# A unit's score products of both heads in one block, and a priority for the sum of its values, in the sparse attention of a decoder

## The chip, the cores and the metric

One Trainium2 chip, one core. The metric is the device time of one execution in microseconds (us), as the median of several runs. Engines are called as in the profile: PE is the matrix engine and PEld its weight loads, DVE the vector engine, ACT the scalar engine, POOL the GpSimd engine.

## The reference, cut to what matters

A decoder of two layers, 512 tokens of 1024 features, all in float32. Each layer has a half-step feed-forward block, a mixer and another half-step feed-forward block. The mixer of the first layer is a gated linear recurrence beside an mLSTM, that of the second is a sparse attention with three branches. Only the attention matters here:

```python
sc = jnp.einsum('bqgrd,bngd->bgrqn', qb, kc)              # compressed keys
p_cmp = masked_softmax(sc, cmp_end[None, :] <= t[:, None])
o_cmp = jnp.einsum('bgrqn,bngd->bqgrd', p_cmp.astype(vc.dtype), vc)
...
ss = jnp.einsum('bqgrd,bgqkd->bgrqk', qb, k_sel)          # selected keys
p_slc = masked_softmax(ss, sel_mask)
o_slc = jnp.einsum('bgrqk,bgqkd->bqgrd', p_slc.astype(v_sel.dtype), v_sel)
...
sw = jnp.einsum('bqgrd,bkgd->bgrqk', qb, k_win)           # a window of 256 keys
p_win = masked_softmax(sw, win_mask)
o_win = jnp.einsum('bgrqk,bkgd->bqgrd', p_win.astype(v_win.dtype), v_win)
out = gb[..., 0:1] * o_cmp + gb[..., 1:2] * o_slc + gb[..., 2:3] * o_win
```

There are 4 groups of 4 heads with 64 features each. With 512 tokens all 8 blocks of 64 keys are selected, so the selected branch is causal attention over all keys.

## The kernel before

Every product in float32 is made of three products of a shorter format: each operand is split into a high and a low half, and high x high, high x low and low x high are added in psum (`mm3`, L175 to L177). PE's order is the order in which the code issues its instructions (`tc.manual_schedule` for PE alone). ACT, DVE and POOL are ordered by a scheduler, by the priorities that follow from the order of the code; `tc.high_priority(offset=...)` puts what it holds that many steps ahead. Each engine then works through its own list in order.

The attention (`nsa`) goes through 32 units: 4 groups `g`, 4 blocks `qb` of 128 queries, and `par`, which picks two of the group's four heads, r = 0 and 1. The work of a unit has two parts.

`scores(u)` makes the scores of both heads. For one head (`both(r)`) these are four products. Two have 128 rows: the high half of the query stands on 64 of them and its low half on the other 64, so that one product against the high half of the keys covers two of the three terms (L942 for the selected keys in `p1`, L943 for the window and the compressed keys together in `p2`). Two have 64 rows: the query's high half against the keys' low half (L944, L945). A `psum()` tile has one of five banks. Then `soft` runs three times, for selected, window and compressed keys: a DVE operation adds the mask and finds the extreme (L932), and an ACT exponential follows (L934), which sums too. `last` also makes the factors `cf` (L952, L953) with which POOL scales the probabilities (L960, L961).

`outputs(u)` multiplies with the values. In a `turn` PE transposes up to four blocks of probabilities into a psum tile `px` (L984), ACT copies it as the high half `ph` (L988), and DVE subtracts for the low half `pl` (L989). In the `add` that belongs to it PE multiplies the values with both (L1000, L1001), with 32 rows for the compressed branch. The `add` comes one turn late. `px` and the accumulator `po` share a pool of three banks. After the last `add` of a unit ACT copies half of `po` to the other half of the partitions (`o`, L1011), DVE adds (L1012), and for every second unit DVE and POOL split the sum (L1016, L1017).

The loop goes over units n: it makes the `outputs` of unit n, and between their turns it hands out the scores of unit n+2 and the fillers, evenly mixed in one list `items`. A filler is three products 512 wide, one step of a projection that the attention needs later (queries and keys first, 69 steps, then 32 steps of the output projection of the first heads). A step of scores is one entry of the list that `scores` returns, so in the kernel before the two heads are two entries with fillers and turns between them:

```python
                    while sc or fl:
                        items += fl[:1] + sc[:1]
                        sc, fl = sc[1:], fl[1:]
```

Of the kernel before, what the change touches and what calls it, by code (L numbers as in the profile page):

```python
# [9 lines left out]
AF = mybir.ActivationFunctionType  # L10
OP = mybir.AluOpType

P = 128
# [41 lines left out]
def build(tc, a, out, stages=("f0a", "ab", "f0b", "f1a", "nsa", "f1b")):  # L55
    nc = tc.nc
    with ExitStack() as ctx:
# [16 lines left out]
        def blk(i, dt, name):  # L74
            return bp.tile([P, BW.get(i, 4 * T)], dt, name=name, tag=f"b{i}")

        def slots(blocks, dt, name):
            return [t[:, s * T:(s + 1) * T] for t in (blk(b, dt, f"{name}{b}") for b in blocks) for s in range(4)]
# [5 lines left out]
        def psum():  # L84
            return pp.tile([P, T], F32, name="ps", bufs=PSB)

        def psum2():
            return pp.tile([P, T], F32, name="pt", bufs=8 - PSB)
# [624 lines left out]
        def nsa(x, nxt):  # L713
# [3 lines left out]
            KH = slots((4,), F32R, "kh")  # L717
            b5, b6, b7 = (blk(b, F32R, f"k{b}") for b in (5, 6, 7))
            KL = [b5[:, m * T:(m + 1) * T] for m in range(2)]
            VC = b5[:, 2 * T:3 * T].rearrange("p (g e) -> p g e", g=NG)  # L720
            kw = [t[:, n * 576:(n + 1) * 576] for t in (b6, b7) for n in range(3)]
            KWH, KWL = kw[0:4], kw[4:6]
# [187 lines left out]
            def scores(u):  # L910
                g, qb, par = u
                qs = slice(qb * P, (qb + 1) * P)
                rr = half[g % 2]
                nk = (qb + 1) * P
                nw = min(3, qb + 1) * P
                w0, wwin, wcmp = (160, 0, 384) if qb == 3 else (0, 32, 0)
                n1, n2 = max(256, nk), max(256, nw + 32)
                mx = tp.tile([P, 2, 3], F32, name="mx", bufs=4)
                sm = tp.tile([P, 2, 3], F32, name="sm", bufs=4)
                cf = tp.tile([P, 2, 3], F32, name="cf", bufs=4)  # L920
                pc = PC[cnt[0] % len(PC)]
                cnt[0] += 1
                Pu = room(u, 2 * (nk + nw))
                pt = [(pc[:, r], Pu[:, r * (nk + nw):r * (nk + nw) + nk], Pu[:, r * (nk + nw) + nk:(r + 1) * (nk + nw)])
                      for r in range(2)]

                def soft(r, b, src, msk):
                    dst = pt[r][b]
                    put = dst
                    if len(msk.shape) == 3:  # L930
                        put, src = (v.rearrange("p (b n) -> p b n", n=P) for v in (dst, src))
                    nc.vector.tensor_tensor_reduce(out=put, in0=src, in1=msk, scale=1.0, scalar=3e38,  # L932
                                                   op0=OP.add, op1=OP.min, accum_out=mx[:, r, b:b + 1])
                    nc.scalar.activation(dst, dst, AF.Exp, scale=-1.0, bias=mx[:, r, b:b + 1],  # L934
                                         accum_out=sm[:, r, b:b + 1])

                def both(r):
                    q = QH[g][2 * r + par]  # L940
                    p1, p2 = psum(), psum()
                    nc.tensor.matmul(p1[:, :n1], q[:, qs], KH[g][:, :n1], start=True, stop=False)  # L942
                    nc.tensor.matmul(p2[:, :n2], q[:, qs], KWH[g][:, w0:w0 + n2], start=True, stop=False)  # L943
                    nc.tensor.matmul(p1[:, :n1], q[rr, qs], KL[g // 2][rr, :n1], start=False, stop=True)  # L944
                    nc.tensor.matmul(p2[:, :n2], q[rr, qs], KWL[g // 2][rr, w0:w0 + n2], start=False, stop=True)  # L945
                    soft(r, 1, p1[:, :nk], MS[:, T - nk:])
                    soft(r, 2, p2[:, wwin:wwin + nw], MS[:, T - nw:] if qb < 2 else MW)
                    soft(r, 0, p2[:, wcmp:wcmp + 32], MC[:, qb])

                def last():  # L950
                    both(1)
                    nc.vector.reciprocal(cf, sm)  # L952
                    nc.vector.tensor_mul(cf, cf, gate[:, qb, 12 * g:12 * g + 12]  # L953
                                         .rearrange("p (r s b) -> p r s b", s=2, b=3)[:, :, par])
                    if qb == 0:
                        nc.vector.tensor_mul(cf[:, :, 0], cf[:, :, 0], valid0)
                    for b in (1, 2):
                        for r in range(2):
                            w = pt[r][b].shape[1]
                            nc.gpsimd.tensor_mul(pt[r][b], pt[r][b], cf[:, r, b:b + 1].to_broadcast([P, w]))  # L960
                    nc.gpsimd.tensor_mul(pc, pc, cf[:, :, 0:1].to_broadcast([P, 2, 32]))  # L961

                probs[u] = pt
                return [lambda: both(0), last]


            def outputs(u):
                g, qb, par = u
                qs = slice(qb * P, (qb + 1) * P)
# [5 lines left out]
                parts, po = {}, []  # L975
# [18 lines left out]
                def add(n):  # L994
                    if n == 0:
                        po.append(psum2())
                    kk, ph, pl = parts.pop(n)
                    for m, (_, v, _) in enumerate(pairs[n]):
                        ms = slice(m * 2 * P, (m + 1) * 2 * P)
                        nc.tensor.matmul(po[0][:, :2 * P], v, ph[:kk, ms], start=n == 0 and m == 0, stop=False)  # L1000
                        nc.tensor.matmul(po[0][:, :2 * P], v, pl[:kk, ms], start=False,  # L1001
                                         stop=n == len(pairs) - 1 and m == len(pairs[n]) - 1)
                    if n < len(pairs) - 1:
                        return
                    if g not in OB:
                        OB[g] = blk((12, 13, 0, 1)[g], F32R, f"o{g}")[:, :4 * T].rearrange("p (k t) -> p k t", k=4)

                    if par == 0:
                        sums[0] = tp.tile([P, 2 * P], F32, name="o", bufs=1)
                    o, own, oth = sums[0], half[par], half[1 - par]  # L1010
                    nc.scalar.activation(o[own], po[0][oth, :2 * P], AF.Copy)  # L1011
                    nc.vector.tensor_add(o[own], po[0][own, :2 * P], o[own])  # L1012
                    if par == 1:
                        oh, ol = OB[g][:, 0:2, qs], OB[g][:, 2:4, qs]
                        o = o.rearrange("p (k t) -> p k t", k=2)
                        nc.vector.tensor_copy(oh, o)  # L1016
                        nc.gpsimd.tensor_sub(ol, o, oh.bitcast(F32))  # L1017
# [97 lines left out]
        last = []  # L1115
# [4 lines left out]
        with tc.manual_schedule(engines=PE_ONLY):  # L1120
            for _ in range(10):
                nc.tensor.matmul(ps[:, :P], ident, ident, start=True, stop=True)
        w0 = [tuple(wp.tile([P, CW], dt, name=nm, bufs=b) for nm, dt, b in
                    (("raw", F32, 2), ("whi", F32R, None), ("wlo", F32R, None))) for _ in range(2)]
# [21 lines left out]
        for n, st in enumerate(stages):  # L1146
# [17 lines left out]
            else:  # L1164
                f = {"f0a": 0, "f0b": 1, "f1a": 2, "f1b": 3}[st]
# [107 lines left out]
```

## Time and profile before

| | before |
| --- | --- |
| median of 3 runs | 2093.01 us |
| runs | 2088.83, 2093.01, 2098.58 us |
| profiled execution | 2106.2 us |
| its span in the trace | 2104.5 us |
| PE busy | 2014.4 us (96%) |
| DVE, ACT, POOL busy | 1383.4 us (66%), 1027.8 us (49%), 280.0 us (13%) |
| mean granted clock of PE | 0.976 |

The profiled execution is one more run, a little longer than those timed. The times in the rows are microseconds from its start. Its attention units run from about 1459 to 1705 us, some 245 us of the whole. Busy time of PE is modelled at the ends of products, so the distance from one start to the next says more than a product's own duration, and a busy PE may still be showing a weight load that isn't hidden.

### The profile page before, as it was taken

What the parts mean: (1) busy time and instruction counts of PE and PEld (TensorE: products, weight loads), DVE (VectorE), ACT (ScalarE), POOL (GpSimd) and SP (SyncE); (2) the same over time, 40 slices, a digit from 0 to 9 for tenths busy, and PEclk for the clock granted to TensorE, in tenths of its full rate; (3) what the DMA queues carried; (4) which work ended last, traced back from release to release, by engine and by line L of the source; (5) the groups of instructions that cost most, each with busy time, mean ns of one, the idle gap of its engine ahead of it and who ended that gap; (6) DMA issues with size and microseconds to landing.
All of it is one profiled execution on the core that took longest, in us unless ns stands there. A gap on an engine that the chain in (4) does not pass through costs nothing.

```text
span 2104.5 us, 30561 instructions
## 1 busy us (share of the span) xinstructions
PE 2014.4 (96%) x11896; PEld 1750.7 (83%) x11896; DVE 1383.4 (66%) x2189; ACT 1027.8 (49%) x1900; POOL 280.0 (13%) x290
## 2 busy tenths in 40 slices
PE   7999899989999999999999999999999999999997
PEld 5889898767888998897889989877777677999896
DVE  6847647488568657475865747433777788657474
ACT  4525436445445435254544525424877755435252
POOL 3000000243020000002000000201646440000002
PEclk9999999999899999999999999999999999999998
DMA  5232322222132323233232323321000032323212
GB/s 172 74 115 83 111 85 76 90 81 90 61 101 80 109 82 111 76 98 108 79 113 83 107 88 99 121 90 60 31 21 17 31 106 80 102 89 111 85 61 85
DMA packets 74737, 182.10 MB, mean 87 GB/s; under 512 B 8416, under 2 KB 9184, under 8 KB 74592
## 3 DMA queue, kind: packets, MB, share of 16 engines
q1 hardware_dynamic: 74448, 180.06, 27.6%
q8 instruction: 93, 1.52, 0.3%
q14 instruction: 52, 0.43, 0.1%
q10 hardware_dynamic: 144, 0.09, 0.0%
HBM read 178.02 MB, written 2.10 MB: 86 GB/s over the span
## 4 chain that ended last, share of the span: by engine, by line
PE 72%; DVE 12%; DMA 6%; issue 5%; ACT 3%; POOL 0%; SPq 0%; DVEq 0%; POOLq 0%; ACTq 0%
PE ps L175 17%; PE ps L176 17%; PE ps L177 17%; DMA r<-wgu 6%; PE pt L176 3%; PE pt L175 3%; PE pt L177 3%; PE px L984 2%; PE pt L779 2%; DVE wlo L319 1%; PE pt L1000 1%; DVE wx L319 1%; DVE r L309 1%; DVE r L310 1%; PE ps L944 1%
## 5 line engine op out<-in xcount | busy, mean ns | idle before, releaser
L169 ACT ACTIVATE whi<-raw 128x1024 fp32r<-128x1024 f32 (+2 forms) x196 | 193.3, 988 | 374.4 <-PE ps L176 254.5
L176 PE MATMUL ps<-h,whi 128*128 128x512 f32 x704 | 278.9, 396 | 0.7 <-DVE h L390 0.7
L175 PE MATMUL ps<-h,whi 128*128 128x512 f32 x704 | 277.8, 395 | 0.7 <-ACT h L389 0.7
L177 PE MATMUL ps<-h,wlo 128*128 128x512 f32 x704 | 277.2, 394 | 0.0
L318 ACT ACTIVATE whi<-r 128x1024 fp32r<-128x1024 f32 (+1 forms) x174 | 165.8, 953 | 211.2 <-PE ps L176 171.0
L170 DVE TENSOR_TENSOR wlo<-raw,whi 128x1024 fp32r<-128x1024 f32 (+2 forms) x166 | 192.5, 1162 | 78.7 <-ACT whi L169 73.8
L116 POOL TENSOR_TENSOR acc<-acc,t 128x512 f32<-128x512 f32 x48 | 76.9, 1603 | 1149.4 <-ACT t L114 1144.2
L457 DVE SCALAR_TENSOR_TENSOR X<-ps,X 128x512 f32<-128x512 f32 x96 | 66.4, 691 | 238.1 <-PE ps L177 238.1
L319 DVE TENSOR_TENSOR wlo<-r,whi 128x1024 fp32r<-128x1024 f32 (+1 forms) x174 | 189.1, 1088 | 28.1 <-ACT whi L318 27.8
L175 PE MATMUL ps<-x,whi 128*128 128x512 f32 x432 | 179.4, 415 | 6.0 <-ACT whi L1133 6.0
L176 PE MATMUL ps<-x,whi 128*128 128x512 f32 x432 | 171.0, 396 | 5.1 <-DVE x L105 4.9
L309 DVE TENSOR_TENSOR r<-r,r 128x1024 f32<-128x1024 f32 x72 | 89.4, 1242 | 130.5 <-DMA r<-wgu 130.4
L177 PE MATMUL ps<-x,wlo 128*128 128x512 f32 x432 | 171.3, 396 | 0.1
L175 PEld LDWEIGHTS ps<-h,whi 128*128 128x128 f32 x704 | 133.7, 190 | 30.8 <-ACT h L389 1.2
L176 PEld LDWEIGHTS ps<-h,whi 128*128 128x128 f32 x704 | 133.7, 190 | 30.7 <-DVE h L390 2.1
L177 PEld LDWEIGHTS ps<-h,wlo 128*128 128x128 f32 x704 | 133.7, 190 | 29.3
L175 PE MATMUL ps<-qB,whi 128*128 128x256 f32 x520 | 145.8, 280 | 2.8 <-ACT u L363 2.8
L177 PE MATMUL ps<-qB,wlo 128*128 128x256 f32 x520 | 145.2, 279 | 1.0 <-DVE wlo L319 1.0
L176 PE MATMUL ps<-qB,whi 128*128 128x256 f32 x520 | 145.3, 279 | 0.1
L319 DVE TENSOR_TENSOR wx<-r,wx 128x1024 fp32r<-128x1024 f32 (+1 forms) x114 | 125.1, 1098 | 23.6 <-ACT wx L318 21.1
L389 ACT ACTIVATE h<-t 128x512 fp32r<-128x512 f32 x88 | 55.4, 630 | 145.3 <-DVE t L371 143.1
L318 ACT ACTIVATE wx<-r 128x1024 fp32r<-128x1024 f32 (+1 forms) x114 | 107.5, 943 | 11.4 <-DVE r L309 9.1
(340 smaller groups left out, 5500.4 us busy)
## 6 DMA issues: line engine op xcount, KB each, us to landing
r<-wgu SPq DMA_DIRECT2D x288, 256.0 KB, 3.7
raw<-wd SPq DMA_DIRECT2D x64, 512.0 KB, 3.5
raw<-wgu SPq DMA_DIRECT2D x30, 512.0 KB, 3.6
raw<-wd SPq DMA_DIRECT2D x32, 384.0 KB, 3.1
raw<-ab_fm SPq DMA_DIRECT2D x21, 512.0 KB, 3.5
raw<-nsa_fm SPq DMA_DIRECT2D x17, 512.0 KB, 3.5
raw<-ab_out SPq DMA_DIRECT2D x8, 512.0 KB, 3.6
raw<-nsa_out SPq DMA_DIRECT2D x16, 256.0 KB, 2.7
```

The source lines that it names most:

```text
L116: nc.gpsimd.tensor_add(acc, acc, sq)
L169: nc.scalar.activation(hi[:, :n], raw[:, :n], AF.Copy)
L170: (eng or nc.vector).tensor_sub(lo[:, :n], raw[:, :n], hi[:, :n].bitcast(F32))
L175: nc.tensor.matmul(ps, wh, xh, start=start, stop=False, skip_group_check=on)
L176: nc.tensor.matmul(ps, wh, xl, start=False, stop=False, skip_group_check=on)
L177: nc.tensor.matmul(ps, wl, xh, start=False, stop=stop, skip_group_check=on)
L309: nc.vector.tensor_add(ra[:, 1:3], ra[:, 0:4:3], rc[:, 3:4].to_broadcast([P, 2, T]))
L318: nc.scalar.activation(hi[:, :m], src, AF.Copy)
L319: nc.vector.tensor_sub(lo[:, :m], src, hi[:, :m].bitcast(F32))
L389: nc.scalar.activation(hh, t2, AF.Copy)
L457: nc.vector.scalar_tensor_tensor(X[i], ps, 0.5, X[i], op0=OP.mult, op1=OP.add)
L779: nc.tensor.matmul(p2[m][:, :155].rearrange("p (g n) -> p g n", g=5), w[:, q * 256 + m * P:q * 256 + (m + 1) * P], tt[:, :, n:n + 8 * 30 + ...
```

## The change

Two edits, both in `nsa`. In `scores`, a unit's two heads are made in one step instead of two, and the products are ordered so that the four with 64 rows stand together: the first head has its 128-row products first, the second head its 64-row products. In `outputs`, the ACT copy and the DVE addition of the sum get a priority 60 steps ahead.

```diff
@@ -939,15 +939,20 @@
                 def both(r):
                     q = QH[g][2 * r + par]
                     p1, p2 = psum(), psum()
-                    nc.tensor.matmul(p1[:, :n1], q[:, qs], KH[g][:, :n1], start=True, stop=False)
-                    nc.tensor.matmul(p2[:, :n2], q[:, qs], KWH[g][:, w0:w0 + n2], start=True, stop=False)
-                    nc.tensor.matmul(p1[:, :n1], q[rr, qs], KL[g // 2][rr, :n1], start=False, stop=True)
-                    nc.tensor.matmul(p2[:, :n2], q[rr, qs], KWL[g // 2][rr, w0:w0 + n2], start=False, stop=True)
+                    for n, f in enumerate((0, 1) if r == 0 else (1, 0)):
+                        a, z = n == 0, n == 1
+                        if f == 0:
+                            nc.tensor.matmul(p1[:, :n1], q[:, qs], KH[g][:, :n1], start=a, stop=z)
+                            nc.tensor.matmul(p2[:, :n2], q[:, qs], KWH[g][:, w0:w0 + n2], start=a, stop=z)
+                        else:
+                            nc.tensor.matmul(p1[:, :n1], q[rr, qs], KL[g // 2][rr, :n1], start=a, stop=z)
+                            nc.tensor.matmul(p2[:, :n2], q[rr, qs], KWL[g // 2][rr, w0:w0 + n2], start=a, stop=z)
                     soft(r, 1, p1[:, :nk], MS[:, T - nk:])
                     soft(r, 2, p2[:, wwin:wwin + nw], MS[:, T - nw:] if qb < 2 else MW)
                     soft(r, 0, p2[:, wcmp:wcmp + 32], MC[:, qb])
 
                 def last():
+                    both(0)
                     both(1)
                     nc.vector.reciprocal(cf, sm)
                     nc.vector.tensor_mul(cf, cf, gate[:, qb, 12 * g:12 * g + 12]
@@ -961,7 +966,7 @@
                     nc.gpsimd.tensor_mul(pc, pc, cf[:, :, 0:1].to_broadcast([P, 2, 32]))
 
                 probs[u] = pt
-                return [lambda: both(0), last]
+                return [last]
 
 
             def outputs(u):
@@ -1008,8 +1013,9 @@
                     if par == 0:
                         sums[0] = tp.tile([P, 2 * P], F32, name="o", bufs=1)
                     o, own, oth = sums[0], half[par], half[1 - par]
-                    nc.scalar.activation(o[own], po[0][oth, :2 * P], AF.Copy)
-                    nc.vector.tensor_add(o[own], po[0][own, :2 * P], o[own])
+                    with tc.high_priority(offset=60):
+                        nc.scalar.activation(o[own], po[0][oth, :2 * P], AF.Copy)
+                        nc.vector.tensor_add(o[own], po[0][own, :2 * P], o[own])
                     if par == 1:
                         oh, ol = OB[g][:, 0:2, qs], OB[g][:, 2:4, qs]
                         o = o.rearrange("p (k t) -> p k t", k=2)
```

The lines move: L942 to L945 become L945, L946, L948 and L949; L984, L988 and L989 become L989, L993 and L994; L1000 and L1001 become L1005 and L1006; L1011 and L1012 become L1017 and L1018.

On PE, at the scores of the last unit of the second group (512 selected keys; `kh4`, `k6` are high halves of keys, `k5`, `k7` low halves, `t1` and `t2` high and low halves of transposed probabilities, `v8` and `v9` values), before:

```order
L942 MATMUL ps_13862<-kh4_11882,q11_12696 128x512
L943 MATMUL ps_13863<-k6_11884,q11_12696 128x416
L944 MATMUL ps_13862<-k5_11883,q11_12696 128x512
L945 MATMUL ps_13863<-k7_11885,q11_12696 128x416
L1000 MATMUL pt_13782<-t1_13825,k5_11883 128x256
L1001 MATMUL pt_13782<-t2_13826,k5_11883 128x256
L984 MATMUL px_13879<-ident_80,pb14_11888 128x128 x4
L175 MATMUL ps_13854<-x0_11658,whi_13850 128x512
L176 MATMUL ps_13854<-x2_11660,whi_13850 128x512
L177 MATMUL ps_13854<-x0_11658,wlo_13851 128x512
L1000 MATMUL pt_13893<-t1_13844,v8_11886 128x256
L1001 MATMUL pt_13893<-t2_13845,v8_11886 128x256
```

and after:

```order
L945 MATMUL ps_13845<-kh4_11882,q11_12740 128x512
L946 MATMUL ps_13846<-k6_11884,q11_12740 128x416
L948 MATMUL ps_13845<-k5_11883,q11_12740 128x512
L949 MATMUL ps_13846<-k7_11885,q11_12740 128x416
L948 MATMUL ps_13857<-k5_11883,q11_12740 128x512
L949 MATMUL ps_13858<-k7_11885,q11_12740 128x416
L945 MATMUL ps_13857<-kh4_11882,q11_12740 128x512
L946 MATMUL ps_13858<-k6_11884,q11_12740 128x416
L1005 MATMUL pt_13795<-t1_13819,k5_11883 128x256
L1006 MATMUL pt_13795<-t2_13820,k5_11883 128x256
L989 MATMUL px_13881<-ident_80,pb14_11888 128x128 x4
L175 MATMUL ps_13701<-x1_11659,whi_13697 128x512
```

The second head's four products, which came after another block of value products and transposes, now stand directly behind the first head's, with the four 64-row products in the middle; the 32-row value products and the transposes `px_13881` come after all eight.

On ACT, from the copy of `o` at the same place on (`pb14` to `pb16` hold probabilities), before:

```order
L1011 ACTIVATE o_13876<-pt_13782 64x256
L988 ACTIVATE t1_13884<-px_13879 128x512
L934 ACTIVATE pb15_11889,sm_13837<-pb15_11889,mx_13836 128x512
L934 ACTIVATE pb15_11889,sm_13837<-pb15_11889,mx_13836 128x384
L934 ACTIVATE pb16_11890,sm_13837<-pb16_11890,mx_13836 128x32
L988 ACTIVATE t1_13903<-px_13898 128x512
L882 ACTIVATE q11_13858<-t1_13859 64x512
L887 ACTIVATE q11_13858<-t1_13859 64x512
L882 ACTIVATE q11_13858<-t1_13859 64x512
L934 ACTIVATE pb15_11889,sm_13837<-pb15_11889,mx_13836 128x512
```

and after, from the copy of the transposes ahead of the scores on:

```order
L993 ACTIVATE t1_13838<-px_13833 128x512
L934 ACTIVATE pb15_11889,sm_13831<-pb15_11889,mx_13830 128x512
L1017 ACTIVATE o_13878<-pt_13795 64x256
L934 ACTIVATE pb15_11889,sm_13831<-pb15_11889,mx_13830 128x384
L934 ACTIVATE pb16_11890,sm_13831<-pb16_11890,mx_13830 128x32
L934 ACTIVATE pb15_11889,sm_13831<-pb15_11889,mx_13830 128x512
L934 ACTIVATE pb15_11889,sm_13831<-pb15_11889,mx_13830 128x384
L934 ACTIVATE pb16_11890,sm_13831<-pb16_11890,mx_13830 128x32
L993 ACTIVATE t1_13886<-px_13881 128x512
L993 ACTIVATE t1_13903<-px_13898 128x512
```

Before, the copies of the transposes `px_13879` and `px_13898` stand ahead of and between the exponentials of the two heads. After, the six exponentials of both heads stand in a row with only the copy of `o` among them, and the copies of `px_13881` and `px_13898` behind the last.

On DVE, at the same place (an L932 row without names reads the accumulator), before:

```order
L932 ISA pb15_11889,mx_13836<-ps_13862,masks_11891 128x512
L932 ISA mx_13836 128x1
L932 ISA pb15_11889,mx_13836<-ps_13863,masks_11891 128x384
L932 ISA mx_13836 128x1
L932 ISA pb16_11890,mx_13836<-ps_13863,pb15_11889 128x32
L932 ISA mx_13836 128x1
L1012 TENSOR_TENSOR o_13876<-pt_13782,o_13876 64x256
L989 TENSOR_TENSOR t2_13885<-px_13879,t1_13884 128x512
L989 TENSOR_TENSOR t2_13904<-px_13898,t1_13903 128x512
```

and after:

```order
L932 ISA pb15_11889,mx_13830<-ps_13845,masks_11891 128x512
L932 ISA mx_13830 128x1
L932 ISA pb15_11889,mx_13830<-ps_13846,masks_11891 128x384
L932 ISA mx_13830 128x1
L932 ISA pb16_11890,mx_13830<-ps_13846,pb15_11889 128x32
L932 ISA mx_13830 128x1
L932 ISA pb15_11889,mx_13830<-ps_13857,masks_11891 128x512
L932 ISA mx_13830 128x1
L1018 TENSOR_TENSOR o_13878<-pt_13795,o_13878 64x256
L932 ISA pb15_11889,mx_13830<-ps_13858,masks_11891 128x384
L932 ISA mx_13830 128x1
```

The addition of `o`, which stood behind the three steps of one head, now stands behind four of six steps and ahead of the last two, and the subtractions for the low halves of the following transposes have moved behind all of them.

## Rows read from the trace of the kernel before

**Rows 1.** Attention's stretch: us; busy PE, PEld, DVE, ACT, POOL (instructions); clock; DMA; GB/s

```profile
1455.00:1710.00 255.00, 244.93 (x1350) 186.16 (x1349) 191.84 (x663) 194.52 (x585) 134.81 (x190) 0.99 0.10 31
```

**Rows 2.** Sums of waits from 1455 to 1705: engine, who waits, releaser; us, times, longest

```profile
PE px L984 <- DVE o L1012: 5.8, 10, 1.1
...
PEld px L984 <- DVE o L1012: 4.9, 7, 1.1
...
PE pt L1000 <- DVE t L989: 1.9, 2, 1.7
```

**Rows 3.** Timeline of PE, scores between fillers: start, duration, line, operation, shapes [idle before]

```profile
1461.43 0.28 PE L942 MATMUL ps<-kh,q 128*128 128x256 f32 x1
1461.55 0.28 PE L943 MATMUL ps<-k,q 128*128 128x256 f32 x1
1461.76 0.38 PE L944 MATMUL ps<-k,q 64*128 64x256 f32 x1
1461.98 0.28 PE L945 MATMUL ps<-k,q 64*128 64x256 f32 x1
1462.19 0.50 PE L175 MATMUL ps<-x,whi 128*128 128x512 f32 x1
1462.53 0.39 PE L176 MATMUL ps<-x,whi 128*128 128x512 f32 x1
1462.76 0.40 PE L177 MATMUL ps<-x,wlo 128*128 128x512 f32 x1
```

**Rows 4.** Timeline of PE around the unit at 1568.87

```profile
1568.87 0.40 PE L942 MATMUL ps<-kh,q 128*128 128x512 f32 x1
...
1569.38 0.50 PE L944 MATMUL ps<-k,q 64*128 64x512 f32 x1
...
1570.22 0.27 PE L1001 MATMUL pt<-t,k 32*128 32x256 f32 x1
...
1572.78 0.66 PE L984 MATMUL px<-ident,pb 128*128 128x128 f32 x4 [0.54 <-DVE o L1012]
1573.19 0.48 PE L942 MATMUL ps<-kh,q 128*128 128x512 f32 x1
...
1574.41 0.50 PE L175 MATMUL ps<-x,whi 128*128 128x512 f32 x1
...
1575.20 0.28 PE L1000 MATMUL pt<-t,v 128*128 128x256 f32 x1
```

**Rows 5.** Timeline of ACT around the same unit

```profile
1570.59 0.38 ACT L1011 ACTIVATE o<-pt 64x256 f32<-64x256 f32 x1 [0.77 <-PE pt L1001]
...
1571.83 0.72 ACT L934 ACTIVATE pb<-pb,mx 128x512 f32<-128x512 f32 x1
...
1572.55 0.60 ACT L934 ACTIVATE pb<-pb,mx 128x384 f32<-128x384 f32 x1
...
1573.53 0.60 ACT L988 ACTIVATE t<-px 128x512 fp32r<-128x512 f32 x1
```

**Rows 6.** Groups by line and form, 1459 to 1705: busy us, mean ns, idle before

```profile
L984 PEld LDWEIGHTS px<-ident,pb 128*128 128x128 f32 x304 | 34.1, 141 | 11.6 <-DVE o L1012 3.8 <-POOL pb L960 2.4 <-POOL pb L961 1.3
```

**Rows 7.** Timeline of DVE around the same unit

```profile
1569.94 1.25 DVE L953 TENSOR_TENSOR cf<-cf,pb 128x6 f32<-128x6 f32 x1
1571.11 0.68 DVE L932 CUSTOM_DVE_ANT_0 pb<-ps,masks 128x512 f32<-128x512 f32 x1
...
1572.31 0.41 DVE L1012 TENSOR_TENSOR o<-pt,o 64x256 f32<-64x256 f32 x1
...
1574.16 0.69 DVE L989 TENSOR_TENSOR t<-px,t 128x512 fp32r<-128x512 f32 x1 [0.84 <-ACT t L988]
```

**Rows 8.** Timeline of PE, two waits for the low half of a transposed block

```profile
1594.74 0.38 PE L1000 MATMUL pt<-t,v 128*128 128x256 f32 x1 [0.19 <-DVE t L989]
...
1667.44 0.39 PE L1000 MATMUL pt<-t,v 128*128 128x256 f32 x1 [1.68 <-DVE t L989]
```

**Rows 9.** Busy time behind the second of them, columns as in rows 1

```profile
1669.60:1673.20 3.60, 3.60 (x13) 2.54 (x12) 2.91 (x9) 1.07 (x3) 1.24 (x2) 0.53 0.23 73
```

## The prediction

> **What bounds the kernel now.** The page's table of busy time comes first: PE is the one full engine. Only the sparse attention of the second layer is touched, so next comes the table of busy time for that stretch, 1455 to 1710 us: PE 244.93 of 255 us, ACT 194.52, DVE 191.84, the granted clock at 0.99 [rows 1]. PE bounds this stage too, but ACT and DVE are at about 76%, and each hands PE an operand several times per unit. So the time of the change is what it takes from or adds to PE's own work, and how often PE waits for ACT and DVE. The sums of waits give today's sizes: PE waits 5.8 us, in ten places, for the sum of a unit's values (`o`, L1012), its load engine another 4.9 us, and 1.9 us for the low half of a transposed block (`t`, L989) [rows 2]. The timeline of PE gives the price of the short products, and the timelines of three engines around one unit give the chain that the change rearranges; there the reader is to see who stands in front of whom.
>
> **The change part by part: the weight loads.** In the timeline of PE a 128-row product of 256 columns behind another starts 0.12 us after it (1461.43 to 1461.55) [rows 3]: its weight load is hidden. From there to the 64-row product it is 0.21 us, to the second 0.22, to the filler behind it 0.21, each 0.09 to 0.10 more; and the filler's first product is 0.34 us from its second (1462.19 to 1462.53), where the second is 0.23 from the third. So a run of two 64-row products shows four loads of about 0.10 us: before it, within it, after it, and one more. A run of four shows six. Two runs of two become one of four in each of 32 units: 8 loads become 6, that is 64 fewer. In 17 places of the order of before, a run stands directly ahead of the 32-row products of the compressed values, which shows the same cost, so the two shared it; in the order of after the 32-row products come behind 128-row ones and pay it alone, two loads each, 34 in all. 64 - 34 = 30 fewer, at 0.10 us: **-3.0 us**. The Trainium skill, page "TensorEngine Tiling (Array Packing)", section "Key Properties", says that a change of the tiling mode drains TensorE. By that rule alone only the changes would cost, 64 fewer of them less 17 that were shared, 47 at 0.10 us or -4.7 us, and the time about 2100, inside the range of the forecast. The row of the second 64-row product, 0.22 us without any change of rows, speaks against that rule being all of it.
>
> **The sum of values.** `o` takes an ACT copy and a DVE addition, and transposes behind it wait, because they take the psum bank that it frees. In the unit at 1568.87 the copy starts at 1570.59, the addition comes behind the softmax steps of the head just scored, at 1572.31, and PE sits idle 0.54 us until 1572.78 [rows 4, 5, 7]. These waits are 5.8 us in PE alone and 10.7 us with those of the load engine [rows 2]. I take a value near the lower end, since the loads mostly run beside PE and only one of 0.141 us [rows 6] stands exposed behind each of the ten: 5.8 + 10 x 0.14 = 7.2 us. With the new priority the addition stands ahead of the last softmax steps of 384 and 32 columns, and in nearly every unit of the new order PE has more work between the last value product and the waiting transposes than the copy and the addition need. I find only three places where it has less, for 0.4 us together: **-6.8 us**. The bounds are -10.7 (both engines' waits, all gone) and 0 (PE waits for the copy instead).
>
> **The copies of transposed blocks, the new cost.** Before, scores of one head were followed by other work, so that ACT had three exponentials, then copies of transposed blocks (L988), then three more. Now all six scores of a unit come at once, the scheduler puts all six exponentials in a row on ACT, and the copies of the transposes that PE issues right behind the scores stand behind them. ACT takes them in that order. I work it out for the unit at 1568.87 (the second order excerpt), in time from its first score product:
> - The 64-row product that ends the first softmax input starts at 0.51 and lasts 0.50, so the softmax step can start at 1.0; in before it started at 2.2 (1571.11), behind an operation of 1.25 us on DVE [rows 4, 7]. The exponential follows 0.72 later (1571.83): at 1.7 to 3.0.
> - Four products and the two 32-row ones reach 1.35 (1568.87 to 1570.22); the other four add about 1.2 (1573.19 to 1574.41) less a load, so the second 32-row product starts at 2.5 and ACT's copy of `o` 0.37 behind it (1570.22 to 1570.59), at 2.9 [rows 4, 5].
> - From one exponential to the next it is 0.72 us behind the one of 512 keys, and 0.98 for those of 384 and 32 together (1571.83, 1572.55, 1573.53) [rows 5]. In the early case the copy of `o` (about 0.4) falls behind the first exponential, and five more follow it (0.98 + 0.72 + 0.98 = 2.7): the copy of the transposed block starts at 6.0. In the late case all six stand there, to 6.6.
> - The low half starts 0.63 later (1573.53 to 1574.16) and takes 0.69 [rows 5, 7]: PE has its operand at 7.3 to 7.9.
> - PE gets there, without waits, in the time between the same two products of before (1570.22 to 1575.20), less the second run of scores (1.2) and the idle 0.54: 3.2 us behind 2.5, and the first product that takes the low half is one product on, at 5.8 [rows 4].
> So PE waits some 1.5 to 2.1 us, where it waited for nothing in before; I take 1.6, since the operation of 1.25 us isn't there in every unit. The same working at each of the 32 units, with exponentials of their widths, gives a wait at 14: seven of the eight units with 512 keys (1.65, 1.65, 1.6, 1.5, 2.1, 1.6, 2.1), three with 384 (1.05, 1.05, and 3.2 in the one where the load of the square root's table falls between the exponentials; it cost 1.68 there in before), one with 256 (0.4) and three with 128 (1.3, 1.1, 0.5). That is 20.8, with rests of a few hundredths elsewhere **+21 us**. The nearest row of such a wait in before that has no table load is 0.19 us, the longest 1.68 [rows 8]; 14 times these bound it at 2.7 and 23.5 us. I take the upper part because the chain is made of measured pieces, and the order fixes it. The old waits of this kind, 1.9 us [rows 2], go or are counted in the 3.2: **-1.9 us**.
>
> **What else moves.** A unit needs four of five psum banks at once, which leaves one to the filler; the softmax steps of the unit before have freed them a microsecond or more earlier wherever I followed it: 0, and a late bank would show as waits of L945 and L946. The prologue loses two of four fillers, which come later: 0, with 1 us as a bound either way, since the first transposes there already wait for POOL and not for a filler. The clock: behind the wait of 1.68 us it was at 0.53 for 3.6 us [rows 9], which costs about 1.7 us. Two of the new waits (2.1) are as long; but they come in two parts, one for the high half and one for the low. I take 0 and keep +3.4 as a bound.
>
> **Sum:** -3.0 - 6.8 - 1.9 + 21 = **+9.3 us**, from 2106.2 us of the profiled execution (span 2104.5) to 2115.5. That execution is 13.2 us above the median of the runs, which is 2093.01; the difference carried over gives **2102 us**.
>
> **The rivals.** (A) *The copies don't bind.* If they find gaps as in before (14 x 0.19 = 2.7 us), the sum is -3.0 - 6.8 - 1.9 + 2.7 = -9.0; with no wait left it is -11.7, so 2081 to 2084. For it: ACT has a quarter of its time free [rows 1]. Against it: that time isn't free in the 4 us behind a block of scores, where six exponentials take 3.4 us. It is on the faster side when the 14 waits together stay under 1.2 us. Chance 0.20.
> (B) *The waits come at full size and bring the clock down.* With DVE as late as in this unit (0.6 us more at 14 places, 8 us) and the two clock dips (3.4) the time is 2102 + 8 + 3.4 = 2113; either alone gives 2105 to 2110. Slower by over 0.5% begins at 2103.5, so it decides as soon as the waits pass 22.2 us. Chance 0.33.
> (C) *The change doesn't do what it says.* If the 64-row products cost as much next to each other (+3.0 against the forecast) and the sum of values still comes late, because its copy waits for a score block that is twice as long (+6.8), the time is 2112. Against it: the addition visibly moves ahead. Chance 0.07.
>
> **How the numbers follow.** The forecast, 2095 to 2104 on its own with waits of 14 to 22 us, has 0.40. A measurement of this kernel can tell about 0.5%, 10.5 us, from no change: faster is under 2082.5, slower over 2103.5. A lies on both sides of the lower bound, so faster gets 0.14 of its 0.20; B and C and a little of the forecast's upper edge are slower: 0.33 + 0.07 + 0.02 = 0.42; same holds the rest, 0.44. The range that leaves out about a tenth on each side is 2082 to 2113.
>
> **What would show it.** In the profile after, ACT's timeline has six exponentials in a row and the copies behind them; PE's idle time before the value products (L1005, L1006), released by DVE `t` L994 or ACT `t` L993, sums to about 20 us; that before the transposes (L989), released by `o` L1018, falls under 1 us; loads that wait on issue ahead of L948 and L949 fall by 30 of 0.1 us. I am wrong if PE's waits for `t` stay under 10 us (A), if the clock in the stage falls under 0.97 (B), or if waits for `o` stay (C).

## The result, and the profile after

| | before | after |
| --- | --- | --- |
| median of 6 runs | 2094.05 us | 2122.41 us |
| range | 2088.83 to 2100.02 us | 2111.31 to 2127.46 us |
| profiled execution | 2106.2 us | 2122.5 us |
| first score product to first product behind the attention | 264.4 us (1459.62 to 1724.04) | 289.2 us (1453.63 to 1742.83) |

The changed kernel is slower: the ratio is 1.0125 with a 95% interval from 1.0096 to 1.0155, some 26 us (28 between the medians). The forecast was 2102 us, and the time lies outside the range of 2082 to 2113. The profiled executions differ by 16 us only, but that one of before was itself 12 us over its median. Between the same two products of each trace, where only the attention lies, it is 24.8 us, which fits the ratio.

The page of after shows that the work is the same: busy time and instructions of each engine.

```profile
PE 2013.4 (95%) x11896; PEld 1750.0 (83%) x11896; DVE 1386.4 (65%) x2189; ACT 1027.3 (48%) x1900; POOL 280.6 (13%) x290
```

In the stage's stretch (columns as in [rows 1]) PE is busy for 226.46 of 255 us where it was 244.93, with ACT and DVE idler too, and the granted clock is 0.96 instead of 0.99, under the 0.97 that the prediction had named as a sign of rival B:

```profile
1455.00:1710.00 255.00, 226.46 (x1223) 173.13 (x1224) 177.00 (x636) 181.10 (x564) 129.30 (x183) 0.96 0.08 24
```

So PE no longer fills the stage. The sums of waits (who waits, for whom; us, times, longest) tell for what. They answer to [rows 2], here from 1445 to 1740 us, since the stage is longer:

```profile
PE pt L1006 <- DVE t L994: 13.1, 20, 1.5
...
PE pt L1005 <- ACT t L993: 11.6, 12, 2.6
...
ACT o L1017 <- PE pt L1006: 12.7, 21, 1.9
...
PE px L989 <- POOL pb L965: 3.0, 2, 2.3
...
PE px L989 <- DVE o L1018: 0.4, 2, 0.2
```

Two sums of before that [rows 2] does not show:

```profile
PE pt L1001 <- DVE t L989: 1.1, 1, 1.1
PE px L984 <- POOL pb L960: 0.6, 1, 0.6
```

The waits for `o` went as forecast, from 5.8 to 0.4 us. The waits for the two halves of transposed blocks went from 3.0 (1.9 and 1.1) to 24.7 us (13.1 and 11.6), and those for POOL from 0.6 to 3.0.

The unit that the prediction worked out stands at 1564.85 in this trace. ACT's timeline there, answering to [rows 5] (the short rows that read the accumulators left out):

```profile
1567.76 0.72 ACT L934 ACTIVATE pb<-pb,mx 128x512 f32<-128x512 f32 x1 [2.21 <-DVE mx L932]
...
1568.60 0.38 ACT L1017 ACTIVATE o<-pt 64x256 f32<-64x256 f32 x1
1569.00 0.62 ACT L934 ACTIVATE pb<-pb,mx 128x384 f32<-128x384 f32 x1
...
1569.62 0.31 ACT L934 ACTIVATE pb<-pb,mx 128x32 f32<-128x32 f32 x1
...
1569.92 0.71 ACT L934 ACTIVATE pb<-pb,mx 128x512 f32<-128x512 f32 x1
...
1570.63 0.60 ACT L934 ACTIVATE pb<-pb,mx 128x384 f32<-128x384 f32 x1
...
1571.22 0.31 ACT L934 ACTIVATE pb<-pb,mx 128x32 f32<-128x32 f32 x1
...
1571.53 1.06 ACT L993 ACTIVATE t<-px 128x512 fp32r<-128x512 f32 x2
```

All six exponentials stand ahead of the copy (L993, two copies in this row), with only `o` among them, as the order had shown. PE, answering to [rows 4]:

```profile
1564.85 0.40 PE L945 MATMUL ps<-kh,q 128*128 128x512 f32 x1
...
1569.49 0.66 PE L989 MATMUL px<-ident,pb 128*128 128x128 f32 x4 [0.22 <-DVE o L1018]
...
1572.16 0.38 PE L1005 MATMUL pt<-t,v 128*128 128x256 f32 x1 [1.31 <-ACT t L993]
1572.88 0.39 PE L1006 MATMUL pt<-t,v 128*128 128x256 f32 x1 [0.34 <-DVE t L994]
```

It arrives at the value products and waits 1.31 us for the high half and 0.34 for the low: 1.65 us, where 1.6 was forecast.

Not every wait comes from ACT's list. The long wait at 1485.66 (its row is in the next section) is for a low half alone:

```profile
1482.39 0.58 ACT L993 ACTIVATE t<-px 128x512 fp32r<-128x512 f32 x1
...
1484.13 0.55 DVE L932 CUSTOM_DVE_ANT_1 pb<-ps,masks 128x384 f32<-128x384 f32 x1
...
1484.92 1.00 DVE L994 TENSOR_TENSOR t<-px,t 128x512 fp32r<-128x512 f32 x2
```

ACT's copy was done at 1482.97, but DVE worked through its softmax steps (L932) first and subtracted from 1484.92 on. It is much the same at four other places (waits of 1.28, 1.12, 1.09 and 0.80 us), where the copy was done 0.9 to 3.0 us before DVE began. These five are 5.8 of the 24.7 us.

### The profile page after: what moved, and what is told of

It is laid out like the page before. It is cut to its first block, busy times and chain, and to the rows that moved or that the text cites. A ratio compares the mean times of both kernels' runs of the same rounds, so it can differ in the third digit from the quotient of the medians.

```text
span 2120.6 us, 30537 instructions
## 1 busy us (share of the span) xinstructions
PE 2013.4 (95%) x11896; PEld 1750.0 (83%) x11896; DVE 1386.4 (65%) x2189; ACT 1027.3 (48%) x1900; POOL 280.6 (13%) x290
## 3 DMA queue, kind: packets, MB, share of 16 engines
q8 instruction: 93, 1.52, 0.3%
## 4 chain that ended last, share of the span: by engine, by line
PE 72%; DVE 13%; DMA 5%; ACT 5%; issue 5%; POOL 0%; SPq 0%; DVEq 0%; POOLq 0%; ACTq 0%
PE ps L175 17%; PE ps L176 17%; PE ps L177 17%; DMA r<-wgu 5%; PE pt L176 3%; PE pt L177 3%; PE pt L175 3%; ACT pb L934 2%; PE pt L779 2%; DVE wlo L319 2%; PE px L989 1%; DVE wx L319 1%; DVE r L309 1%; DVE t L994 1%; PE pt L1006 1%
## 5 line engine op out<-in xcount | busy, mean ns | idle before, releaser
L319 DVE TENSOR_TENSOR wlo<-r,whi 128x1024 fp32r<-128x1024 f32 (+1 forms) x174 | 189.0, 1087 | 28.6 <-ACT whi L318 28.3
```

The source lines that it names most:

```text
L319: nc.vector.tensor_sub(lo[:, :m], src, hi[:, :m].bitcast(F32))
```

## Where the 24.8 us come from

The idle times in PE's timeline from the first score product to the first product behind the attention add up to 28.3 us, against 9.7 in before: **18.6 us**. The granted clock has a second part. In before one stretch was at 0.53 [rows 9], 1.7 us lost. After has four such stretches (columns as in [rows 1], the clock is the third from the end):

```profile
1464.00:1470.50 6.50, 6.50 (x21) 4.94 (x20) 2.84 (x16) 3.10 (x14) 1.76 (x5) 0.51 0.01 4
1573.50:1577.00 3.50, 3.50 (x16) 3.12 (x14) 0.41 (x1) 0.42 (x2) 2.58 (x4) 0.54 0.00 0
1645.00:1649.00 4.00, 4.00 (x17) 2.90 (x15) 1.12 (x2) 1.10 (x3) 3.99 (x5) 0.57 0.01 4
1682.50:1689.00 6.50, 6.39 (x21) 4.99 (x21) 4.07 (x16) 1.87 (x6) 3.42 (x5) 0.50 0.00 0
```

That is 0.49 x 6.5 + 0.46 x 3.5 + 0.43 x 4.0 + 0.50 x 6.5 = 9.8 us lost, **8.1 us** more. Of the two levels of the clock, 1.2 and 2.4 GHz, the engine was at the lower one for most of these rows. Each comes behind one of PE's long waits: two of them behind idle 2.29 and 2.63 us, two behind 1.31 and 1.52 us with another 0.34 behind these. But a single wait of 1.50 us at 1485.66 had none behind it, and neither had one of 1.51 us at 1706.91 with another of 0.37 behind it:

```profile
1461.94 1.40 PE L989 MATMUL px<-ident,pb 128*128 128x128 f32 x4 [2.29 <-POOL pb L965]
...
1485.66 0.38 PE L1006 MATMUL pt<-t,v 128*128 128x256 f32 x1 [1.50 <-DVE t L994]
...
1643.83 0.39 PE L1005 MATMUL pt<-t,v 128*128 128x256 f32 x1 [1.52 <-ACT t L993]
...
1682.20 0.38 PE L1005 MATMUL pt<-t,k 32*128 32x256 f32 x1 [2.63 <-ACT t L993]
...
1706.91 0.38 PE L1005 MATMUL pt<-t,v 128*128 128x256 f32 x1 [1.51 <-ACT t L993]
```

18.6 + 8.1 = 26.7 us, so PE's own work, together with what doesn't show as idle, is 1.9 us less than before. That remainder hides two parts of opposite sign, to which the experiments on the short products come back.

## The experiments

Theory Q: the copies of transposed blocks queue behind six exponentials, PE waits for them, and the clock falls behind the long waits. Rival P: the priority for the sum of values is the loss, because ACT stands waiting for PE with exponentials behind it (ACT's waits for `o` are 12.7 us in 21 places; in before they were 12.8 in 14, which speaks against it already). Rival M: the merged step itself takes cover away on PE. Each ratio is against the kernel before, on the same chip.

**The pairing alone.** The changed kernel with the priority taken out:

```diff
-                    with tc.high_priority(offset=60):
-                        nc.scalar.activation(o[own], po[0][oth, :2 * P], AF.Copy)
-                        nc.vector.tensor_add(o[own], po[0][own, :2 * P], o[own])
+                    nc.scalar.activation(o[own], po[0][oth, :2 * P], AF.Copy)
+                    nc.vector.tensor_add(o[own], po[0][own, :2 * P], o[own])
```

> The changed kernel without the priority for the sum of values; the score block is as in the changed kernel. In ACT's order the copy of o now stands behind all six exponentials in most units, and the copies of transposed blocks behind that. Theory Q (copies queue behind six exponentials): PE's waits for t stay at 20 to 30 us, waits for o come on top, 5 to 15 us, since two copies are late instead of one; 2125 to 2145 us. Rival P (the priority makes ACT wait for PE with the exponentials queued behind it, and that is the loss): near the kernel before, 2088 to 2100 us, waits for t under 10 us.

Measured: 2127.26 us, 1.0133 (1.0102 to 1.0163). The loss is there without the priority, so P falls. Its sums of waits:

```profile
PE px L989 <- DVE o L1017: 22.0, 16, 2.7
...
PE pt L1005 <- ACT t L993: 8.0, 8, 2.2
...
PE pt L1006 <- DVE t L994: 6.9, 11, 1.3
```

Q had the total about right (36.9 us) and the split wrong: with the copy of `o` behind all exponentials too, most of the waiting is done for `o`, and the copy of the transposed block then comes in its shadow.

**The priority alone**, the same two lines in the kernel before.

> The kernel before with the priority alone; scores in two steps as before. Theory Q: the waits for o (5.8 us of PE, 4.9 us of its loads) fall under 2 us and nothing else grows by more than 2 us: 4 to 8 us faster than before, 2086 to 2091 us. Rival P: ACT waits for the value products with exponentials behind them, waits for t grow to over 10 us, 2100 to 2115 us.

Measured: 2097.82 us, 0.9981 (0.9966 to 0.9995), with PE's waits for `o` at 0.5 us and for `t` at 4.4. This edit is a gain of 1 to 7 us by itself.

**The copies ahead of the exponentials.** The changed kernel, with PE's order as it is but for a few products at the stage's end, and the copy on ACT and the subtraction on DVE both moved ahead:

```diff
-                    nc.scalar.activation(ph[:kk, :w], px[:kk, :w], AF.Copy)
-                    nc.vector.tensor_sub(pl[:kk, :w], px[:kk, :w], ph[:kk, :w].bitcast(F32))
+                    with tc.high_priority(offset=80):
+                        nc.scalar.activation(ph[:kk, :w], px[:kk, :w], AF.Copy)
+                        nc.vector.tensor_sub(pl[:kk, :w], px[:kk, :w], ph[:kk, :w].bitcast(F32))
```

> The changed kernel, and the ACT copy and the DVE subtraction of a transposed block get a priority 80 steps ahead, so that the copies stand between the exponentials again; PE's order is that of the changed kernel. Theory Q: PE's waits for t fall from 25 us to under 8 us, and the stretches of low clock behind them (1572, 1645) go; 2092 to 2104 us. Rival P: nothing of note, 2115 to 2125 us. Rival M (the loss is the merging of the two steps on PE itself, with less other work between scores and what needs them): waits move to other places, 2112 to 2125 us.

Measured: 2095.73 us, 0.9975 (0.9957 to 0.9992), and once more, beside the runs that follow:

> The kernel with the copies of transposed blocks ahead once more, on the chip of the three others, so that they can be compared with it. As before: 2 to 10 us under the kernel before.

2093.25 us, 0.9968 (0.9947 to 0.9989). The whole loss of 1.25% is gone and some 5 to 7 us more, with the merged step in place. So M falls, and Q is shown in this form: it was the order on the engines behind PE. The edit moves the copy and the subtraction together, so ACT's part and DVE's (5.8 us of waits, by the trace) aren't parted by a run. In the second of these traces ACT has copies (now L994) between the exponentials of the same unit, and PE's waits for `t` are 1.3 us. A new wait has come, since the later exponentials hand POOL its factors later:

```profile
1560.16 0.72 ACT L934 ACTIVATE pb<-pb,mx 128x512 f32<-128x512 f32 x1 [1.74 <-DVE mx L932]
...
1561.62 0.60 ACT L994 ACTIVATE t<-px 128x512 fp32r<-128x512 f32 x1 [0.20 <-PE px L989]
1562.11 0.61 ACT L934 ACTIVATE pb<-pb,mx 128x384 f32<-128x384 f32 x1
...
1563.72 0.58 ACT L994 ACTIVATE t<-px 128x512 fp32r<-128x512 f32 x1
1564.20 0.61 ACT L934 ACTIVATE pb<-pb,mx 128x384 f32<-128x384 f32 x1
```

```profile
PE px L989 <- POOL pb L965: 7.1, 8, 2.3
```

**Less of it.** With 24 steps instead of 80 the exponentials stand mostly in threes.

> The changed kernel with the copies of transposed blocks 24 steps ahead instead of 80. In ACT's order the exponentials stand mostly in threes with a copy between, so a copy waits for three of them at most (1.0 to 1.7 us) and the factors that POOL needs come earlier than with 80 steps. Theory Q: waits for t between those of the changed kernel (24.7 us) and of 80 steps (2 us), nearer the lower, 2 to 8 us; waits for POOL fall from 7 us to 3 to 5; the time within 4 us of the kernel with 80 steps, 4 to 12 us under the kernel before. If six in a row are not the point but any queueing, waits for t stay over 12 us, at the kernel before or above.

Measured: 2103.30 us, 1.0013 (0.9995 to 1.0030). The waits lie between, nearer the lower, as expected of Q:

```profile
PE pt L1007 <- DVE t L995: 6.5, 14, 1.2
...
PE px L989 <- POOL pb L965: 2.9, 3, 2.3
...
PE pt L1006 <- ACT t L994: 1.8, 1, 1.8
```

The time missed its expectation: PE was idle 12.2 us in the stage, and 5.1 us went to the clock. Neither of the two offsets serves both sides: with 24 steps the waits for `t` are still 8.3 us, with 80 those for POOL are 7.

**The first part.** The changed kernel with a second `fill()` behind each of the first two score steps:

```diff
                     for f in scores(u):
                         f()
                         fill()
+                        fill()
```

> The changed kernel with two fillers instead of one behind each of the first two units' scores, which gives the first part back the four fillers of before. Theory Q with the prologue counted: the wait of 2.29 us for POOL at the first transposes and the low clock of 6.5 us behind it (3.4 us lost) go, 4 to 6 us faster than the changed kernel, 2114 to 2119 us. If the wait moves with the fillers, within 2 us of the changed kernel, 2120 to 2124 us.

Measured: 2112.20 us, 1.0068 (1.0041 to 1.0096), about 12 us under the changed kernel's ratio, more than expected. The wait for POOL at the first transposes falls from 2.29 to 0.71 us, the whole idle time by 3.8 to 24.4 us only; but the granted clock is at 0.99 over the stretch:

```profile
1455.00:1710.00 255.00, 229.82 (x1288) 176.65 (x1286) 180.91 (x643) 185.77 (x572) 131.48 (x189) 0.99 0.09 28
```

A single stretch of low clock is left, behind the wait of 2.62 us. So in these two profiled executions the rest of the gain is clock: the waits of 1.31 and 1.51 us with 0.34 behind them are there in this run too, and the clock stayed up. The execution shown is the fastest of five (2108.45 to 2125.60 us), so how often it stays up is open. With the copies ahead as well, the extra fillers bring nothing more:

> Copies of transposed blocks ahead and two fillers behind each of the first two score blocks. If the wait of 2.29 us for POOL and the low clock behind it are one cause of their own, as the run with four fillers alone suggests, this is 3 to 6 us under the kernel with the copies ahead, 7 to 14 us under the kernel before. If the low clock moves to the next wait, within 2 us of the kernel with the copies ahead.

Measured: 2094.35 us, 0.9966 (0.9941 to 0.9992), the same as without. The wait of 2.29 us is gone, and the low clock stands behind a later wait for POOL:

```profile
1664.00:1675.00 11.00, 10.21 (x41) 7.86 (x42) 5.07 (x15) 5.25 (x14) 7.01 (x11) 0.69 0.08 25
```

The second run with the copies ahead had low clock at both places, 8.5 us lost in all, where the first had it behind the 2.29 us alone, 3.4 us lost, with nearly the same waits. So a single execution doesn't tell what one wait costs.

With 24 steps they bring 0.0034 in the ratio, 9 us between the medians:

> The same with two fillers behind each of the first two score blocks. The wait of 2.29 us for POOL at the first transposes goes to under 1 us; the whole idle time of the stage under 7 us, 8 to 14 us under the kernel before. If the low clock only moves on to a later wait, as with 80 steps, within 2 us of the run with 24 steps alone.

Measured: 2094.31 us, 0.9979 (0.9956 to 1.0002), idle 8.3 us, one short stretch of low clock. That is less than the 8 to 14 us under the kernel before that were expected, and more than the low clock only moving on would have given.

**The order of the short products.** The prediction had a run of four 64-row products show six weight loads, and the gain at 3.0 us. With the copies ahead, and both heads with their 128-row products first:

```diff
-                    for n, f in enumerate((0, 1) if r == 0 else (1, 0)):
+                    for n, f in enumerate((0, 1)):
```

> Copies of transposed blocks ahead, a unit's two heads still in one step, but each head with its 128-row products first, so that the 64-row products stand in two runs of two. By the rows (a run of two shows four loads of 0.10 us, a run of four six, the run that stands directly ahead of a 32-row product shares two): 3.0 us above the kernel with the copies ahead. By the rule that only a change of rows costs: 4.7 us above. If the order of the products is worth nothing: within 1 us of it.

Measured: 2103.65 us, 1.0013 (0.9993 to 1.0034), 10.4 us above the run with the 64-row products together on the same chip. All three expectations were too small. The trace of after shows why; a unit at 1472.22, in PE's timeline:

```profile
1472.34 0.29 PE L946 MATMUL ps<-k,q 128*128 128x288 f32 x1
1472.56 0.38 PE L948 MATMUL ps<-k,q 64*128 64x256 f32 x1
1472.78 0.29 PE L949 MATMUL ps<-k,q 64*128 64x288 f32 x1
1472.91 0.28 PE L948 MATMUL ps<-k,q 64*128 64x256 f32 x1
1473.03 0.29 PE L949 MATMUL ps<-k,q 64*128 64x288 f32 x1
1473.25 0.39 PE L945 MATMUL ps<-kh,q 128*128 128x256 f32 x1
1473.47 0.30 PE L946 MATMUL ps<-k,q 128*128 128x288 f32 x1
```

From start to start it is 0.22, 0.22, 0.13, 0.12, 0.22 and 0.22 us. The load of 0.10 us shows twice where the rows change from 128 to 64, twice where they change back, and not inside the run. In the run with the rows apart, each change again shows two:

```profile
1508.03 0.28 PE L946 MATMUL ps<-k,q 128*128 128x256 f32 x1
1508.24 0.38 PE L948 MATMUL ps<-k,q 64*128 64x256 f32 x1
1508.46 0.28 PE L949 MATMUL ps<-k,q 64*128 64x256 f32 x1
1508.67 0.39 PE L945 MATMUL ps<-kh,q 128*128 128x256 f32 x1
1508.89 0.28 PE L946 MATMUL ps<-k,q 128*128 128x256 f32 x1
```

(1508.24 to 1508.46, 1508.67 to 1508.89, and so on: all about 0.22.) So a run of two and a run of four both show four loads. A unit goes from 8 to 4, not from 8 to 6: 32 x 4 = 128 fewer, less the 34 that the 32-row products now show alone, 94 x 0.10 = 9.4 us.

The traces bear this out in two ways. In the stage the products change their number of rows 177 times in before and 130 times in after, 185 times in the run with the rows apart and 132 times with the rows together; at 0.2 us a change that is 9.4 and 10.6 us. And the stage's time less PE's idle rows and less what the clock took leaves 264.4 - 9.7 - 1.7 = 253.0 us in before and 266.9 - 7.9 - 5.1 = 253.9 with the rows apart, but 258.4 - 9.6 - 3.4 = 245.4 and 262.2 - 8.7 - 8.5 = 245.0 in the two runs with the copies ahead: 8 to 9 us.

The same edit in the changed kernel itself, with that kernel beside it:

> The changed kernel once more, on the chip of the next one. As before: 1.0 to 1.6% over the kernel before, with several stretches of low clock behind PE's longest waits.

> The changed kernel with both heads in one step, but each head with its 128-row products first, so that the 64-row products stand in two runs of two. In the run with the copies ahead this order was worth about 9 us, as if each change of rows cost two loads of 0.10 us and a run of four no more than a run of two: 94 loads. Here PE waits for the copies in most units, so that PE's slower work should be taken back by shorter waits there: PE's own work 9 us more, its waits for t 3 to 8 us less, the time 2 to 7 us above the changed kernel. If a run of four shows six loads, as the prediction had it: PE's own work 3 us more, waits 1 to 3 us less, the time within 2 us of the changed kernel.

Measured: 2129.83 us, 1.0121 (1.0100 to 1.0142), and 2137.14 us, 1.0162 (1.0139 to 1.0184): 7.3 us above it, just over the upper end of what the new count gives, and outside the 2 us of the old one, though the two intervals still touch. The trace of the first shows the changed kernel's waits again (25.3 us for `t`); no comparable trace of the second is at hand, so whether its waits shortened stays open.

**Two steps, both priorities.** Scores as before, the sum of values 60 and the copies 80 steps ahead:

> The kernel before, scores in two steps, with both priorities: the sum of values 60 steps and the copies of transposed blocks 80 steps ahead. Theory Q: in two steps the copies were hardly late, so the second priority adds 0 to 3 us to what the first gave (about 4 us), 4 to 8 us under the kernel before. If the merged step is worth something of its own beside the loads, this is over 5 us slower than the kernel with the copies ahead; by the loads alone, 3 us slower, less 5 us for the wait in the first part that it does not have.

Measured: 2102.99 us, 1.0001 (0.9982 to 1.0020). Q's expectation failed: the copies were hardly late here, and their priority costs 7.2 us of waits for POOL in eleven places, which takes back what the other priority gave. Against the kernel with the copies ahead it is 9.7 us slower, about what the short products are worth (9.4), and by the same sum its stage holds 265.7 - 10.0 - 1.7 = 254.0 us of PE's own work, as before.

Best of all runs are the three with ratios of 0.9966 to 0.9975: the whole change with the copies of transposed blocks 80 steps ahead, with or without the extra fillers, 5 to 7 us faster than the kernel before. The difference between them is inside their intervals, and so is that to the run with 24 steps and extra fillers (0.9979) and to the priority for `o` alone (0.9981): that the pairing with the copies ahead beats the priority alone isn't shown.

## Why the prediction was wrong, point by point

- **The copies of transposed blocks: right in mechanism for ACT, near in size partly by luck.** +21 us was forecast, less 1.9 of the old waits; the waits went from 3.0 to 24.7 us, +21.7. (The old ones were 3.0, not 1.9: the one of 1.11 us at 1695.39 was left out.) The worked unit waited 1.65 us against 1.6, and the one with the table load 2.63 against 3.2. But there were 20 places with a wait rather than 14, 1.2 us each on average rather than 1.5, and 5.8 us of it came of DVE's own list, where the working had DVE wait for ACT only.
- **The sum of values: right.** The idle time for `o` fell from 5.8 to 0.4 us, with 0.4 left as forecast.
- **The clock: the step that failed most.** "Two of the new waits (2.1) are as long; but they come in two parts ... I take 0 and keep +3.4 as a bound." It was +8.1 us in the profiled execution. Waits in two parts (1.31 and 0.34) brought it too, so splitting them was no reason. Neither length nor splitting decides it in these traces: 1.51 with 0.37 behind it brought none, and in the repeat of the changed kernel a single 1.97 at the place of the 1.50 brought 3.4 us at the lower level. What decides stays open. Runs of the changed kernel go from 2111.31 us at a mean clock of 0.982 to 2127.46 us at 0.972.
- **The first part: failed.** "0, with 1 us as a bound either way". The first transposes waited 2.29 us for POOL instead of 0.56, because the scores of two units came with two fillers less between them (with these back it was 0.71), and the low clock behind it cost 3.2 us (counted above).
- **The weight loads: the mechanism was misread.** "A run of four shows six" took the load within a run of two for a cost of every product in the run; it is the second load of the change. By the count of changes the term was -9.4 us instead of -3.0, and the two pairs of runs gave 10.4 and 7.3. The rule of the Trainium skill, page "TensorEngine Tiling (Array Packing)", section "Key Properties", that changing the tiling mode drains TensorE, was set aside on the row of the second product. The runs agree with it in that only the changes cost; a drain as such no run shows. The page gives no price; here it is two loads, 0.2 us a change, so that the 47 changes which the prediction counted by this rule are 9.4 us and not 4.7.
- **What was left out: a wait costs more than its idle row.** By the terms so far the stage should have grown by 18.6 + 8.1 - 9.4 = 17.3 us; it grew by 24.8. The 7.5 us between are a remainder. The sum of the section on the short products puts a size to it: the changed kernel holds 289.2 - 28.3 - 9.8 = 251.1 us of PE's work where the same products with the copies ahead took 245, some 6 us more with 37 waits than with 12. Why isn't shown. A likely part is that an idle row counts from the modelled end of the product ahead, which lies 0.16 us behind the point where the next could start (0.39 against a pitch of 0.23), and that a load behind a wait shows as well: as an estimate, some 0.26 us for each of about 22 more waits would be 5.7 us.
- **The forecast as a whole.** The sum came to +9.3. The terms taken at zero or left out (clock 8.1, first part 1.7, the cost of a wait beyond its row 7.5) were all on the losing side, some 17 us together; the loads gave back 6.4 more than forecast. The range ended at rival B, at 2113 with a chance of 0.33, which had the clock but not the other two. It priced two dips of 1.7 us where three stretches were added and two of the four were twice as long (3.2 us), and its other 8 us, for a late DVE, came only as the 2.6 us by which the waits passed the forecast.

## What to carry to other kernels

Here, merging two steps on the full engine merged their followers on the others as well: read the order of the engines that come next, all of them, and ask which operand the full engine needs soon after the merged block stands behind all of it. Such an edit and a priority for that operand belong together: the changed kernel is 1.25% slower without it and 0.3% faster than before with it. The waits cost more here than their idle rows, by a low clock behind some of them (8.1 us more than before) and by some 6 us that show as neither, so a forecast of waits should not take these two at nothing.

## What the runs showed of the hardware

- A change between products with 128 and 64 rows shows two weight loads of about 0.10 us, in either direction, behind a run of two 64-row products as behind one of four; inside a run of four the loads are hidden (0.12 and 0.13 us from start to start at 256 and 288 columns).
- The granted clock was at 0.50 to 0.57 over 3.5 to 6.5 us behind idle times of 2.29 and 2.63 us and of 1.31 and 1.52 us with 0.34 more. Such idle times weren't followed by it at every place (1.51 us with 0.37 more, in the same trace), nor in every kernel, nor twice alike in two executions of one kernel with nearly the same waits (3.4 and 8.5 us lost).
